# First mixer of a hybrid decoder: another order of the small products of the head pairs

## The chip, the cores and the metric

The kernel runs on one core of a Trainium2 chip. The metric is the device time of one execution in microseconds. Before the change it is 1539.14 us, the median of 3 runs (1536.59 to 1540.36).

## What is computed

The reference is one inference step of a two-layer trunk for two groups of requests that share the weights: one prompt of 512 positions and 8 sequences of 4 new positions each, 544 columns in all, 1024 channels. Every layer is a mixer and a feed-forward part, each with a layer norm behind it. The first mixer has two halves, a convolution module on 512 channels and a recurrence on the other 512, in 8 heads of 64:

```
p = x @ w_in                          # 1024 -> conv slice | recurrence slice
for each head and position t:         # the state s is 64 x 64
    sa = -s @ kk_t
    s  = s * decay_t + outer(sa, kk_t * a_t) + outer(v_t, k_t)
    y_t = s @ r_t
out = concat(ya, norm(y) * g) @ w_out
```

## The kernel before, in words

Channels lie on the 128 partitions, positions along the free axis. Weights stream in as f32, are split into a rounded high part and a rest (L262 on ScalarE, L170 on VectorE or GpSimd), and each projection is three products of split operands. All projections go through one helper, so their products have the line L192; L170 and L167 are helpers of VectorE and GpSimd (`tt`, `stt`), L164 one of ScalarE.

The recurrence of the 512 prompt positions is computed in 8 chunks of 64 positions. Two heads share the 128 partitions, one on partitions 0 to 63, the other on 64 to 127 (`HS[0]`, `HS[1]`): a head pair, of which there are four. Per pair there are these parts:

- `pair_in`: projections and element-wise work give `ar`, `kb` and `v`.
- `pair_front`, with `wkv_front` (L709) and `wkv_solve`. L725 multiplies `kb` and `ar` of each of 8 chunks and 2 heads: a contraction over the 64 partitions of one head, 128 rows and 128 columns of output. Four chunks fill one bank of PSUM, and VectorE multiplies the bank by a mask into `xa` and `xk`. SyncE's queue takes `xa` to DRAM (L730, `dx`), one transfer per half, and the solve reads it back in another layout (L770, `xb`). GpSimd inverts small triangles (`stmp`, `mm`), and the result goes through DRAM (L783, `dm`) into `mn` (L787). Meanwhile the front makes transposes and `R`.
- `pair_mid`, with `wkv_mid` (L791): products with `mn` (L801, the first that needs the solve), L809, L816, L823, L831, and last L840, which multiplies the inverse `n64` with `R`. In L840 the contraction and the output of a chunk both lie on the half `HS[c % 2]`. ScalarE copies the result into `R` (L842) and `wv` (L844). Then `wkv_tail` makes the chunks' transfer matrices (L859, L865).
- `pair_out`, with `wkv_scan` (L873): the states run through the chunks one after the other (L882), then L889 multiplies each chunk's state with `qt`, on partition half `H` for contraction and output, and a norm and a gate follow.

PSUM is allocated by kinds of bank: 3 "mm", 1 "wi", 1 "wf", 2 "wo", 1 "wb". Before the change the front uses "wf" alone, the middle and the tail use "wo", and L889 "wi". A bank is given out again when its last reader is through.

The parts are generators that `weave` (L172) takes turns with: for instance the front of pair 1 beside the middle of pair 0, the inputs of pair 2, a convolution projection and convolution taps on VectorE. Each generator has an offset of priority (front -6, middle and output -4, taps +8; lower goes first), and a scheduler fixes each engine's order before the program runs. An engine works through its order and waits where an operand or a bank is not there yet.

An f32 product is two instructions on TensorE, so every product counts twice in the profile.

Of the kernel before, what the change touches and what calls it, by code (L numbers as in the profile page):

```python
# [15 lines left out]
P = 128  # L16
# [76 lines left out]
HS = (slice(0, 64), slice(64, 128))  # L93
# [31 lines left out]
class Kernel:  # L125
# [583 lines left out]
    def wkv_front(self, d, dx):  # L709
        nc, gp = self.nc, self.gp  # L710
        ar, kb, v = d["ar"], d["kb"], d["v"]

        xa = d["xa"] = gp.tile([P, 2, 8, 64], F32, name="xa", tag="xa", bufs=XA)
        xk = d["xk"] = gp.tile([P, 2, 8, 2, 64], F32, name="xk", tag="xk", bufs=2)
        R = d["R"] = gp.tile([P, 2, 4, 2, 64], F32, name="R", tag="R", bufs=2)
        wv = d["wv"] = gp.tile([P, 2, 4, 2, 64], F32, name="wv", tag="wv", bufs=2)
        m3 = self.con0("ma").rearrange("p (a t) -> p a t", a=2).unsqueeze(1).broadcast_to([P, 4, 2, 64])
        idn = self.con("ident")
        flat = lambda t: t.rearrange("p a t -> p (a t)")
        for hd in range(2):  # L720
            for g in range(2):
                pa = self.bank([P, 4, 2, 64], "wf")
                for i in range(4):
                    c = 4 * g + i
                    nc.tensor.matmul(pa[:, i], lhsT=flat(kb[HS[hd], c // 2, c % 2]), rhs=ar[HS[hd], :, c], start=True,  # L725
                                     stop=True)
                for a, t in enumerate((xa[:, hd, 4 * g:4 * g + 4], xk[:, hd, 4 * g:4 * g + 4, 0])):
                    self.tt(t, pa[:, :, a], m3[:, :, a], ALU.mult)
            for c2 in range(2):
                nc.sync.dma_start(out=dx[HS[c2], hd * 4:hd * 4 + 4, :],  # L730
                                  in_=xa[HS[c2], hd].rearrange("p (cp c2) t -> p cp c2 t", c2=2)[:, :, c2])
            yield

        pt = self.bank([P, 4, 2, 64], "wf")
        for j in range(1, 4):
            nc.tensor.transpose(flat(pt[:, j]), v[:, 128 * j - 64:128 * j + 64], idn)
        nc.tensor.matmul(flat(pt[HS[1], 0]), lhsT=v[:, 0:64], rhs=idn, start=True, stop=True)
        nc.tensor.transpose(flat(pt[HS[0], 0]), v[:, 448:512], idn)
        for c2 in range(2):
            nc.scalar.copy(wv[HS[1 - c2], c2], pt[HS[1 - c2]])  # L740
        yield
        pb = self.bank([P, 2, 4, 64], "wf")
        for c, c2, cp, j, hd, S, O in self.blocks():
            nc.tensor.matmul(pb[S, hd, cp], lhsT=xa[O, hd, c], rhs=wv[O, c2, j, hd], start=True, stop=True)
        nc.scalar.copy(R[:, :, :, 1], pb)
        yield
        pt = self.bank([P, 4, 2, 64], "wf")
        for cp in range(4):
            nc.tensor.transpose(flat(pt[:, cp]), flat(ar[:, 0, 2 * cp:2 * cp + 2]), idn)
        nc.scalar.copy(R[:, :, :, 0], pt.rearrange("p cp hd c -> p hd cp c"))  # L750
        for g in range(2):
            pt = self.bank([P, 4, 2, 64], "wf")
            for i in range(4):
                c = 4 * g + i
                nc.tensor.transpose(flat(pt[:, i]), flat(kb[:, c // 2, c % 2]), idn)
            nc.scalar.copy(xk[:, :, 4 * g:4 * g + 4, 1], pt.rearrange("p c hd t -> p hd c t"))
        yield
# [33 lines left out]
    def wkv_mid(self, d):  # L791

        nc, gp = self.nc, self.gp
        mn = self.mn.rearrange("p (hd cp) a t -> p hd cp a t", hd=2)
        xa, R, wv = d["xa"], d["R"], d["wv"]
        S0, S1 = [slice(h, h + 32) for h in (0, 64)], [slice(h, h + 32) for h in (32, 96)]
        new = lambda nm, w, tag, bufs: gp.tile([P, 2, 4, w], F32, name=nm, tag=tag, bufs=bufs)
        all_ = list(self.blocks())
        pz = self.bank([P, 2, 4, 64], "wo")
        for c, c2, cp, j, hd, S, O in all_:  # L800
            nc.tensor.matmul(pz[S, hd, cp], lhsT=xa[S, hd, c], rhs=mn[S, hd, cp, 0], start=True, stop=True)  # L801
        z = new("z", 64, "s2k", S2)
        f = lambda t: t.rearrange("p hd cp t -> p (hd cp) t")
        self.tt(f(z), f(pz), self.con0("off16").unsqueeze(1).broadcast_to([P, 8, 64]), ALU.mult)
        yield

        pi = self.bank([P, 2, 4, 32], "wo")
        for c, c2, cp, j, hd, S, O in all_:
            nc.tensor.matmul(pi[S0[c2], hd, cp], lhsT=mn[S0[c2], hd, cp, 1, 0:32], rhs=z[S0[c2], hd, cp, 0:32],  # L809
                             start=True, stop=True)  # L810
        ni = new("ni", 32, "ni", 1)
        for q in S0:
            self.tt(ni[q], pi[q], mn[q, :, :, 0, 0:32], ALU.add)
        pn = self.bank([P, 2, 4, 64], "wo")
        for c, c2, cp, j, hd, S, O in all_:
            nc.tensor.matmul(pn[S, hd, cp], lhsT=z[S, hd, cp], rhs=mn[S, hd, cp, 1], start=True, stop=True)  # L816
        n64 = new("n64", 64, "n64", 1)
        self.tt(n64, pn, mn[:, :, :, 1], ALU.add)
        yield

        px = self.bank([P, 2, 4, 32], "wo")
        for c, c2, cp, j, hd, S, O in all_:
            nc.tensor.matmul(px[S1[c2], hd, cp], lhsT=xa[S0[c2], hd, c, 32:64], rhs=ni[S0[c2], hd, cp], start=True,  # L823
                             stop=True)
        x = new("x", 32, "nx", 1)
        for q in S1:
            nc.scalar.copy(x[q], px[q])
        yield
        po = self.bank([P, 2, 4, 32], "wo")
        for c, c2, cp, j, hd, S, O in all_:  # L830
            nc.tensor.matmul(po[S0[c2], hd, cp], lhsT=x[S1[c2], hd, cp], rhs=n64[S1[c2], hd, cp, 32:64], start=True,  # L831
                             stop=True)
        for q in S0:
            nc.scalar.copy(n64[q, :, :, 32:64], po[q])
        yield
        for h in range(2):
            pw = self.bank([P, 4, 2, 64], "wo")
            for c, c2, cp, j, hd, S, O in all_:
                if hd == h:
                    nc.tensor.matmul(pw[S, j].rearrange("p a t -> p (a t)"), lhsT=n64[S, h, cp],  # L840
                                     rhs=R[S, h, cp].rearrange("p a t -> p (a t)"), start=True, stop=True)
            nc.scalar.copy(R[:, h, :, 0], pw[:, :, 0])  # L842
            for c2 in range(2):
                nc.scalar.copy(wv[HS[c2], c2, :, h], pw[HS[c2], :, 1])  # L844
        yield
# [27 lines left out]
    def wkv_scan(self, p, d):  # L873
        nc, gp = self.nc, self.gp
        qt, gt, xp, pend = d["qt"], d["gt"], d["xp"], d["pend"]
        st = gp.tile([P, 9, 64], F32, name="st", tag="st", bufs=1)
        pss = self.bank([P, 8, 64], "wb")
        nc.gpsimd.tensor_copy(st[:, 1], xp[:, 0, 0])
        for c in range(1, 8):
            c2, cp = c % 2, c // 2  # L880
            for H in HS:
                nc.tensor.matmul(pss[H, c], lhsT=gt[H, c2, cp], rhs=st[H, c], start=True, stop=True)  # L882
            self.stt(st[:, c + 1], pss[:, c], pend[:, c:c + 1], xp[:, c2, cp], ALU.mult, ALU.add)
            yield
        nc.scalar.dma_start(out=self.O["wkv_p"][p], in_=st[:, 8])
        py = self.bank([P, 8, 64], "wi")
        for c in range(1, 8):
            for H in HS:
                nc.tensor.matmul(py[H, c], lhsT=st[H, c], rhs=qt[H, c % 2, c // 2], start=True, stop=True)  # L889
        y = d["y"][:, 64:NP]  # L890
        self.tt(y, py[:, 1:8].rearrange("p c t -> p (c t)"), y, ALU.add)
        yield
# [977 lines left out]
```

## Time and profile before

| | |
|---|---|
| median of 3 runs | 1539.14 us |
| the profiled execution | 1547.23 us, its span 1545.5 us |
| TensorE busy | 1449.8 us, 94% of the span |
| VectorE, ScalarE, GpSimd busy | 66%, 40%, 23% |
| mean granted TensorE clock | 0.951 of full speed |
| first mixer with its small products | roughly 40 to 370 us of the span |

The profile is of one execution. PE is TensorE, DVE VectorE, ACT ScalarE, POOL GpSimd, SP SyncE, which here only issues DMAs. An engine's share is an average over stages with different limits, so the views by stage are read for the stretch in which the change lies. Durations of neighbouring products on TensorE overlap, as they are pipelined; the distance of their starts is what a product takes of the engine's time.

### The profile page before, as it was taken

The page shows a single profiled execution, that of the slowest core. Times are in us where ns is not written, and L with a number is a line of the kernel's source. Part 1 is how long each engine was busy: PE and PEld are TensorE (multiplying, and loading weights), DVE is VectorE, ACT ScalarE, POOL GpSimd, SP SyncE. Part 2 cuts the span into 40 slices and gives each one's busy share as a digit, 9 for nine tenths or more (in the row PEclk, how much of TensorE's full clock was granted, in tenths as well). Part 3 has the DMA queues.
Part 4 walks back from the last instruction along what each step waited for, and adds up shares of the span by engine and source line. Part 5 has one row for each costly group of instructions (what it writes and reads, how often), then busy time and mean ns, then how long its engine had stood idle before and what let it go on. Part 6 is the DMA issues. An engine that isn't in the chain of part 4 may idle for free.

```text
span 1545.5 us, 31297 instructions
## 1 busy us (share of the span) xinstructions
PE 1449.8 (94%) x12064; PEld 1378.1 (89%) x12064; DVE 1016.7 (66%) x2513; ACT 617.1 (40%) x1407; POOL 353.5 (23%) x492
## 2 busy tenths in 40 slices
PE   7999999789799999999999789899999999999996
PEld 6987887577789999999999778799899999999996
DVE  6698786776979955558994856554675555554335
ACT  5444252251364444442233526443454444442222
POOL 1252542621540100003551611103420000000102
PEclk9999999799899999999999789899999999999997
DMA  5222123111313232225563278632222222233321
GB/s 189 74 63 70 39 53 101 22 38 57 101 44 117 87 123 89 90 86 165 175 184 111 98 209 218 176 101 97 74 63 95 89 87 87 89 91 86 84 68 58
DMA packets 128341, 152.43 MB, mean 99 GB/s; under 512 B 46513, under 2 KB 71857, under 8 KB 127937
## 3 DMA queue, kind: packets, MB, share of 16 engines
q1 hardware_dynamic: 105232, 120.11, 26.5%
q10 hardware_dynamic: 20800, 22.46, 4.7%
q0 software_dynamic: 2160, 7.87, 1.6%
q8 instruction: 95, 1.56, 0.4%
q14 instruction: 54, 0.43, 0.1%
HBM read 128.17 MB, written 22.22 MB: 97 GB/s over the span
## 4 chain that ended last, share of the span: by engine, by line
PE 71%; DVE 10%; DMA 6%; POOL 5%; issue 4%; ACT 3%; SPq 1%; ACTq 0%; POOLq 0%; DVEq 0%
PE ps_mm L192 61%; PE ps_wk L192 3%; POOL mm L170 2%; DVE xres L170 2%; POOL stmp L170 2%; DVE xres L167 1%; DVE wlo L170 1%; DMA tm<-dk 1%; PE ps_wf L725 1%; DMA ye<-dy 1%; DVE ln_t L167 1%; DMA xin<-in_xT 1%; POOL s5a L170 1%; PE ps_wk L1089 1%; ACT xres L164 1%
## 5 line engine op out<-in xcount | busy, mean ns | idle before, releaser
L192 PE MATMUL ps_mm<-xh,whi 128*128 128x256 f32 (+1 forms) x2016 | 492.2, 298 | 22.5 <-ACT whi L262 6.8
L192 PE MATMUL ps_mm<-xl,whi 128*128 128x256 f32 (+1 forms) x2016 | 493.5, 296 | 4.7 <-DVE xl L167 3.6
L192 PE MATMUL ps_mm<-xh,wlo 128*128 128x256 f32 (+1 forms) x2016 | 490.5, 295 | 0.0
L262 ACT CAST whi<-wraw 128x512 fp32r<-128x512 f32 x380 | 230.8, 611 | 517.9 <-PE ps_mm L192 445.6
L170 DVE TENSOR_TENSOR wlo<-wraw,whi 128x512 fp32r<-128x512 f32 x350 | 256.6, 735 | 271.3 <-ACT whi L262 266.2
L192 PEld LDWEIGHTS ps_mm<-xh,whi 128*128 128x128 f32 x2016 | 353.6, 195 | 30.3 <-ACT whi L262 7.1
L192 PEld LDWEIGHTS ps_mm<-xl,whi 128*128 128x128 f32 x2016 | 357.0, 195 | 13.6 <-issue 5.9
L192 PEld LDWEIGHTS ps_mm<-xh,wlo 128*128 128x128 f32 x2016 | 354.9, 194 | 4.6 <-issue 3.9
L192 PE MATMUL ps_mm<-fh,whi 128*128 128x256 f32 (+1 forms) x704 | 154.2, 290 | 0.0
L192 PE MATMUL ps_mm<-fl,whi 128*128 128x256 f32 (+1 forms) x704 | 153.2, 289 | 0.0
L192 PE MATMUL ps_mm<-fh,wlo 128*128 128x256 f32 (+1 forms) x704 | 153.0, 288 | 0.0
L192 PEld LDWEIGHTS ps_mm<-fh,whi 128*128 128x128 f32 x704 | 115.4, 188 | 1.8 <-issue 1.6
L192 PEld LDWEIGHTS ps_mm<-fh,wlo 128*128 128x128 f32 x704 | 115.7, 188 | 0.1
L192 PEld LDWEIGHTS ps_mm<-fl,whi 128*128 128x128 f32 x704 | 115.7, 188 | 0.0
L167 DVE SCALAR_TENSOR_TENSOR c<-ps_mm,cols,c 128x254 f32<-128x254 f32 (+3 forms) x264 | 98.3, 394 | 0.3
L167 DVE SCALAR_TENSOR_TENSOR cacc<-uext,cols,cacc 128x512 f32<-128x512 f32 x120 | 94.8, 790 | 2.5 <-ACT cacc L164 1.6
L170 POOL TENSOR_TENSOR ln_s<-xres 128x256 f32<-128x256 f32 (+1 forms) x8 | 10.8, 1368 | 312.6 <-DVE xres L170 312.6
L170 DVE TENSOR_TENSOR c<-ps_mm,c 128x256 f32<-128x256 f32 (+1 forms) x88 | 35.4, 436 | 59.2 <-PE ps_mm L192 54.8
L170 POOL TENSOR_TENSOR wlo<-wraw,whi 128x512 fp32r<-128x512 f32 x30 | 41.4, 1388 | 81.1 <-ACT whi L262 78.4
L192 PE MATMUL ps_mm<-yh,whi 128*128 128x256 f32 (+1 forms) x240 | 58.6, 299 | 0.3 <-ACT sg L164 0.3
L192 PE MATMUL ps_mm<-yl,whi 128*128 128x256 f32 (+1 forms) x240 | 57.4, 294 | 0.0
L192 PE MATMUL ps_mm<-yh,wlo 128*128 128x256 f32 (+1 forms) x240 | 57.4, 293 | 0.0
(374 smaller groups left out, 2085.6 us busy)
## 6 DMA issues: line engine op xcount, KB each, us to landing
wraw<-in_w_up SPq DMA_DIRECT2D x176, 256.0 KB
wraw<-in_w_down SPq DMA_DIRECT2D x80, 256.0 KB
wraw<-in_w_in_ab SPq DMA_DIRECT2D x44, 256.0 KB
wraw<-in_w_out_c SPq DMA_DIRECT2D x21, 256.0 KB
wraw<-in_w_out_ab SPq DMA_DIRECT2D x16, 256.0 KB
df<-s5a ACTq DMA_DIRECT2D x8, 512.0 KB
gx<-dg POOLq DMA_DIRECT2D x8, 512.0 KB, 4.9
tm<-dk SPq DMA_DIRECT2D x64, 64.0 KB
```

The costliest lines, as they stand in the source:

```text
L164: return self.nc.scalar.activation(out, in_, f, **k)
L167: return self.nc.vector.scalar_tensor_tensor(out, a, s, b, op0, op1)
L170: return (eng or self.nc.vector).tensor_tensor(out, a, b, op=op)
L192: ins = self.nc.tensor.matmul(*a, **k)
L262: self.nc.scalar.copy(hi, src)
L725: nc.tensor.matmul(pa[:, i], lhsT=flat(kb[HS[hd], c // 2, c % 2]), rhs=ar[HS[hd], :, c], start=True, stop=True)
L1089: gate = nc.tensor.matmul(pq[:, 4 * i + j:4 * i + j + 1], lhsT=t[:, b - P:b], rhs=self.con("ones")[:, 0:1], start=t is ts[0], stop=t is ts ...
```

## The change

Three places get another order. In `wkv_front` the two heads take turns, chunk by chunk, each with a bank of its own ("wf" and "wo"), so a round is eight products instead of four and there are two rounds per pair instead of four; both heads' transfers of `xa` to `dx` are issued in the second round. In `wkv_mid` the products of both heads are issued chunk by chunk into two "wo" banks, and the copies follow after all of them. In `wkv_scan` the chunks go in twos: two on one partition half, then the same two on the other.

```diff
-        for hd in range(2):
-            for g in range(2):
-                pa = self.bank([P, 4, 2, 64], "wf")
-                for i in range(4):
-                    c = 4 * g + i
+        for g in range(2):
+
+            pas = [self.bank([P, 4, 2, 64], t) for t in ("wf", "wo")]
+            for i in range(4):
+                c = 4 * g + i
+                for hd, pa in enumerate(pas):
                     nc.tensor.matmul(pa[:, i], lhsT=flat(kb[HS[hd], c // 2, c % 2]), rhs=ar[HS[hd], :, c], start=True,
                                      stop=True)
+            for hd, pa in enumerate(pas):
                 for a, t in enumerate((xa[:, hd, 4 * g:4 * g + 4], xk[:, hd, 4 * g:4 * g + 4, 0])):
                     self.tt(t, pa[:, :, a], m3[:, :, a], ALU.mult)
-            for c2 in range(2):
-                nc.sync.dma_start(out=dx[HS[c2], hd * 4:hd * 4 + 4, :],
-                                  in_=xa[HS[c2], hd].rearrange("p (cp c2) t -> p cp c2 t", c2=2)[:, :, c2])
+                if g:
+                    for c2 in range(2):
+                        nc.sync.dma_start(out=dx[HS[c2], hd * 4:hd * 4 + 4, :],
+                                          in_=xa[HS[c2], hd].rearrange("p (cp c2) t -> p cp c2 t", c2=2)[:, :, c2])
             yield
...
-        for h in range(2):
-            pw = self.bank([P, 4, 2, 64], "wo")
-            for c, c2, cp, j, hd, S, O in all_:
-                if hd == h:
-                    nc.tensor.matmul(pw[S, j].rearrange("p a t -> p (a t)"), lhsT=n64[S, h, cp],
-                                     rhs=R[S, h, cp].rearrange("p a t -> p (a t)"), start=True, stop=True)
+        pws = [self.bank([P, 4, 2, 64], "wo") for _ in range(2)]
+        for c, c2, cp, j, hd, S, O in all_:
+            nc.tensor.matmul(pws[hd][S, j].rearrange("p a t -> p (a t)"), lhsT=n64[S, hd, cp],
+                             rhs=R[S, hd, cp].rearrange("p a t -> p (a t)"), start=True, stop=True)
+        for h, pw in enumerate(pws):
             nc.scalar.copy(R[:, h, :, 0], pw[:, :, 0])
...
-        for c in range(1, 8):
+        for cs in ((1, 2), (3, 4), (5, 6), (7,)):
             for H in HS:
-                nc.tensor.matmul(py[H, c], lhsT=st[H, c], rhs=qt[H, c % 2, c // 2], start=True, stop=True)
+                for c in cs:
+                    nc.tensor.matmul(py[H, c], lhsT=st[H, c], rhs=qt[H, c % 2, c // 2], start=True, stop=True)
```

## Rows read from the trace of the kernel before

**Rows 1.** The page: busy time of each engine; TensorE in 40 slices, in tenths

```profile
PE 1449.8 (94%) x12064; PEld 1378.1 (89%) x12064; DVE 1016.7 (66%) x2513; ACT 617.1 (40%) x1407; POOL 353.5 (23%) x492
...
PE   7999999789799999999999789899999999999996
```

**Rows 2.** The chain of waits, 60 to 370 us: shares of that stretch

```profile
by line: PE ps_mm L192 28.9%; POOL mm L170 8.0%; POOL stmp L170 7.5%; issue 4.8%; PE ps_wf L725 4.5%; SPq L787 2.9%; PE ps_wo L840 2.5%; DMA dm<-mm 2.2%; DMA dx<-xa 1.8%; DMA mn<-dm 1.8%; PE ps_wo L801 1.8%; ACT L164 1.7%; PE ps_wb L882 1.6
```

**Rows 3.** Table by stage: length, busy us of each engine (instructions), granted clock, DMA

```profile
180.00:210.00 30.00, 30.00 (x356) 25.04 (x354) 26.77 (x50) 13.52 (x30) 8.37 (x13) 0.92 0.16 46
...
270.00:300.00 30.00, 21.33 (x234) 14.21 (x234) 25.81 (x55) 6.44 (x14) 21.09 (x39) 0.73 0.13 25
```

**Rows 4.** Waits of TensorE, 60 to 345 us: total, times, longest

```profile
PE ps_wo L801 <- DMA mn<-dm: 12.7, 5, 3.5
```

**Rows 5.** Groups of TensorE by shape: count, busy us, mean ns, idle before

```profile
L725 PE MATMUL ps_wf<-ar,kb 64*128 64x128 f32 x128 | 19.5, 288 | 0.0
...
L840 PE MATMUL ps_wo<-R,n 64*64 64x128 f32 x128 | 10.3, 302 | 0.0
...
L889 PE MATMUL ps_wi<-qt,st 64*64 64x64 f32 x112 | 6.0, 225 | 0.0
```

**Rows 6.** Timeline of TensorE, two front rounds: start, length, line, count

```profile
65.83 0.93 PE L725 MATMUL ps_wf<-ar,kb 64*128 64x128 f32 x6
...
70.22 0.30 PE L192 MATMUL ps_mm<-xl,whi 128*128 128x288 f32 x1
70.35 0.29 PE L192 MATMUL ps_mm<-xh,wlo 128*128 128x288 f32 x1
70.57 1.16 PE L725 MATMUL ps_wf<-ar,kb 64*128 64x128 f32 x8
71.66 0.40 PE L192 MATMUL ps_mm<-xh,whi 128*128 128x288 f32 x1
71.90 0.30 PE L192 MATMUL ps_mm<-xl,whi 128*128 128x288 f32 x1
```

**Rows 7.** Timeline of TensorE: whole groups of L840, L816 and L889

```profile
202.63 1.96 PE L840 MATMUL ps_wo<-R,n 64*64 64x128 f32 x30
...
251.70 1.20 PE L816 MATMUL ps_wo<-mn,z 64*64 64x64 f32 x32
...
272.20 1.03 PE L889 MATMUL ps_wi<-qt,st 64*64 64x64 f32 x28
```

**Rows 8.** Timeline of TensorE: last two front rounds of pair 0 and pair 3

```profile
76.22 1.16 PE L725 MATMUL ps_wf<-ar,kb 64*128 64x128 f32 x8
...
83.42 1.16 PE L725 MATMUL ps_wf<-ar,kb 64*128 64x128 f32 x8
...
264.71 1.16 PE L725 MATMUL ps_wf<-ar,kb 64*128 64x128 f32 x8
...
268.75 1.16 PE L725 MATMUL ps_wf<-ar,kb 64*128 64x128 f32 x8
```

**Rows 9.** Timelines of VectorE and SyncE: last xa multiply and its transfers, pair 0

```profile
85.29 0.42 DVE L170 TENSOR_TENSOR xa<-ps_wf,cons 128x256 f32<-128x256 f32 x1
...
85.73 1.25 SPq L730 DMA_DIRECT2D dx<-xa  x2
```

**Rows 10.** Timeline of ScalarE: copies behind L840, first and second head

```profile
203.75 0.37 ACT L842 COPY R<-ps_wo 128x256 f32<-128x256 f32 x1 [0.89 <-PE ps_wo L840]
...
204.79 0.37 ACT L842 COPY R<-ps_wo 128x256 f32<-128x256 f32 x1
```

**Rows 11.** Timelines of TensorE and VectorE: a front round between two middle groups

```profile
193.59 0.46 PE L823 MATMUL ps_wo<-ni,xa 32*32 32x32 f32 x16
...
195.51 1.16 PE L725 MATMUL ps_wf<-ar,kb 64*128 64x128 f32 x8
...
197.48 0.71 PE L831 MATMUL ps_wo<-n,x 32*32 32x32 f32 x32
...
197.79 0.41 DVE L170 TENSOR_TENSOR xk<-ps_wf,cons 128x256 f32<-128x256 f32 x1
```

## The prediction

> **What bounds the kernel now.** I read the page first. TensorE is busy for 94% of the span, VectorE for 66%; in the slices the 9s of TensorE break between slice 7 and slice 10, roughly 270 to 425 us [rows 1]. The products that the change touches all lie in the first mixer, so next comes the chain of waits of that stretch, 60 to 370 us. The plain projections (L192) hold the largest share; L725, the first of the three edited products, holds 4.5% of 310 us, some 14 us; the rest of the chain is the triangular solve on GpSimd (stmp and mm) with the transfers around it [rows 2]. The table by stage shows the two regimes: TensorE busy 30.00 of 30 us at 180 to 210, but 21.33 of 30 at a granted clock of 0.73 at 270 to 300 [rows 3]. The list of waits names the one stall of weight inside: the first product of the middle part (L801) waits 12.7 us in 5 waits, at most 3.5 each, for the solve's result to land [rows 4]. So up to about 270 us a nanosecond saved on TensorE counts, unless the solve of the head pair comes no earlier; then it returns as waiting at L801.
>
> **The change, part by part.** The listing by shape gives the size: 128 instructions for L725, 128 for L840, 112 for L889 (an f32 product is two of them, so 64, 64 and 56 products) [rows 5].
>
> *Front products (L725).* Now a round is four products, 8 instructions, all on one half of the array's rows, into one bank. Such a round lasts 1.16 us, one of 6 instructions 0.93, so one more costs (1.16 - 0.93) / 2 = 0.115 us. What it takes out of the stream of projections is more: from the projection before it (70.35) to the second one behind it (71.90) is 1.55 us, where two steps of 0.13 would do, so 1.29 us; 8 x 0.115 = 0.92 of it is the products and 0.37 the going in and out [rows 6]. There are 16 rounds, 20.6 us. Afterwards there are 8 rounds of 16 instructions, whose neighbours use opposite halves of the rows and different banks. The trace shows no two products that differ in rows alone, so I bound it. From below in gain: nothing overlaps, a round costs 1.29 + 0.92 = 2.21 us, and 8 save 20.6 - 17.7 = 2.9. From above: it goes as the nearest row does, L840 today, whose neighbours differ in rows and in columns: 30 instructions in 1.96 us, (1.96 - 0.27) / 29 = 0.058 each [rows 7]; then 16 take 0.27 + 15 x 0.058 = 1.14 us, what 8 take now, and 8 rounds save 8 x 1.29 = 10.3. I take 10.3, as L840 is the same width of 128 on the same half of the rows; only its weights are half as wide.
>
> But the second bank is of kind "wo", which the middle part of the pair before also uses. Where none is free, the second head's products come after the first's and the round costs 2.21. Pair 0 has no middle part beside it; of the six rounds of pairs 1 to 3 I take two so, 2 x 0.92 = +1.8 us (bounds 0 and 5.5). VectorE's 32 multiplies of this part stay as many.
>
> *The transfers of head 0* move from the second round to the last, so four of them, not two, stand in SyncE's queue behind the last multiply, ahead of the reloads of the solve and of weight loads: two take 1.25 us, so +1.25, and the last xa multiply comes third instead of first, 2 x 0.42 = +0.84. Against it, two rounds go: the last one lay 7.2 us behind the one before in pair 0 (76.22 to 83.42) and 4.0 in pair 3 (264.71 to 268.75) [rows 8, 9]. The solve's input is thus ready about 2 to 5 us earlier per pair, and TensorE about 2 us earlier: I leave the wait at L801 as it is, 0. That stall is what is late next: the bounds are -6 (about half of the 12.7 goes) and +5 (4 x 1.25, if the rounds win nothing).
>
> *Middle products (L840).* Today opposite halves alternate in one bank; afterwards two products of the same half follow each other, then two of the other, in two banks. The trace has this order, with half the width, in L816: 32 instructions in 1.20 us, (1.20 - 0.22) / 31 = 0.0316 each, against (1.03 - 0.22) / 27 = 0.0300 for L889, which alternates at the same width [rows 7]. So 0.0016 more, twice that at full width: 128 x 0.0032 = +0.4 us. The bounds: no overlap left at all, 128 x (0.115 - 0.058) = +7.3; below, a break inside a group saved per pair, 4 x 0.37 = -1.5. The Trainium skill, page "TensorEngine Tiling (Array Packing)", section "Gotcha 1: PSUM Pressure", says that different row tiles cannot use one bank at the same time. By that rule today's L840, in one bank, would run one by one and a bank each would win 7.3 us; the 0.058 us a step of L840 stands against it, so the sum holds no such gain and the rule's result is a rival with a small chance.
>
> ScalarE's copies out of the first bank (L842, L844; about 1 us from 203.75 to the second set at 204.79) now begin after nearly all 32 instructions instead of 16, 16 x 0.058 = 0.9 us later [rows 10]; who waits is the tail (L859), with projections before it: 0, bounds 0 and 4 x 0.9 = 3.7.
>
> *Output products (L889).* The same step from turns to twos, one bank: 112 x 0.0016 = +0.2; if the overlap went, 112 x 0.029 = +3.2 (half of L840's 0.057).
>
> The sum: -10.3 + 1.8 + 0.4 + 0.2 = -7.9 us. It is made against the profiled execution, 1547.23 us (span 1545.5), which stands 8.1 above the median; a term of this size changes by nothing that matters between them, so 1539.14 - 7.9 = 1531.2 us.
>
> **The rivals.** *Row halves alone do not overlap*, or a "wo" bank is so seldom free that the order is not what the code says. Then -2.9 + 0.6 = -2.3: 1536.8. For it: no row shows such a pair. Against: the pairs of L840 and L889.
>
> *The wait for the solve goes too.* The input is earlier by more than TensorE is, and half of the 12.7 us goes: -7.9 - 6 = -13.9: 1525.2. For it: the distance of the rounds. Against: the solve on GpSimd stands between other work.
>
> *Slower: the front holds a bank of the middle.* The place is "wo", two banks. A round of the front holds its bank until VectorE has read it: 195.51 to 198.20 now, 2.7 us, and 3.5 with two more multiplies ahead; with one bank left, each product group of the middle waits for the evacuation of the last, and TensorE, which works in order, stands. At 2.5 us in each of six rounds that is +15: 1539.1 - 7.9 + 15 = 1546.2. It decides from 7.9 / 6 = 1.3 us a round. Against it: between two groups of the middle lie 3.4 us of other work (194.05 to 197.48) [rows 11], in which the bank comes free.
>
> *The twos lose their overlap.* Both upper bounds come true, 7.3 + 3.2 = 10.5 in place of 0.6: -10.3 + 1.8 + 10.5 = +2.0: 1541.1. Against: the 0.0316 of L816 in that order. The Trainium skill, page "TensorE: Matmul & The Clock Gate", section "Part 3: Packing small matmuls", says that a weight load overlaps a running product only if its row group differs, which speaks against the twos; by that rule this rival would be the likeliest, and L816 does not bear it out.
>
> *A bank each wins in the middle products*, because sharing one holds them apart today: -7.3 in place of +0.4, so -10.3 + 1.8 - 7.3 + 0.2 = -15.6: 1523.5. Against: the step of 0.058 in one bank, half of the 0.115 of products that don't overlap. This is the rule of the page on array packing named above.
>
> **How the numbers follow.** Forecast 0.55; row halves alone do not overlap 0.18; the wait goes too 0.11; the middle's bank held 0.10; the twos 0.04; a bank each wins 0.02. A measurement of this kernel tells about 0.3%, 4.6 us, from no change: below 1534.5 is faster, above 1543.8 slower. The forecast's own bounds put about 0.47 of its 0.55 below 1534.5; with 0.11, 0.02 and 0.03 of the first rival's, 0.63 faster. Slower is most of the held bank's case: 0.09. The rest, 0.28, is the same. The range 1523 to 1541 holds the forecast, the first rival and most of the second; it leaves out the held bank's case, half of the twos' and the edge of the gains.
>
> **What would show it.** Right: L725 in groups of up to 16 in about 1.2 us; two rounds per pair; L840 as 32 in about 2 us, L889 as 28 in about 1.1; the waits at L801 near 12; the first mixer ends about 8 us earlier. Wrong: 16 of L725 in about 2.1 us (row halves); a new wait of TensorE at L809, L816, L823, L831 or L840 for an xa or xk multiply (the bank); L840 or L889 at twice the time (the twos); L801 waiting longer than now, with dx issued later (the transfers).

## The result, and the profile after

The changed kernel takes 1553.45 us (median, 1550.56 to 1556.67) against 1539.75 us for the kernel before (1536.59 to 1544.0), measured side by side: a ratio of 1.0084, 95% interval 1.0059 to 1.0109. It is slower by some 13 us, where 8 us less had been forecast, and it lies outside the range. The profiled execution of before stood some 8 us above its median and that of after (1550.56 us) 3 below, so the two traces differ by 3.3 us only; they are compared stretch by stretch, not end to end.

The page of the changed kernel, busy time and TensorE in 40 slices, answers to [rows 1]:

```profile
PE 1439.2 (93%) x12064; PEld 1372.8 (89%) x12064; DVE 1012.0 (65%) x2513; ACT 616.6 (40%) x1407; POOL 343.5 (22%) x492
...
PE   7989897789879999999999789899899999999996
```

TensorE is busy for 10.6 us less (1439.2 against 1449.8) and the kernel is longer all the same: the engine is idle instead. Between 77 and 271 us three of the slices of TensorE lose one or two tenths. Where the loss is made can be told by counting the projections (L192) through: the 1400th starts at 419.0 us, where it started at 409.0, so some 10 us are lost in the first mixer. The table by stage, with the two stretches of [rows 3] and one between (length, busy us of each engine, granted clock, share of the DMA engines, GB/s):

```profile
180.00:210.00 30.00, 30.00 (x352) 26.59 (x351) 29.59 (x57) 12.71 (x29) 10.20 (x15) 1.00 0.25 71
240.00:270.00 30.00, 19.95 (x186) 16.31 (x184) 28.26 (x66) 4.02 (x7) 4.40 (x6) 0.66 0.30 88
270.00:300.00 30.00, 20.00 (x306) 15.04 (x304) 15.64 (x34) 8.71 (x22) 18.46 (x41) 0.83 0.11 20
```

and the row of 240 to 270 us in the kernel before:

```profile
240.00:270.00 30.00, 28.31 (x353) 24.29 (x354) 20.66 (x49) 7.32 (x17) 6.01 (x8) 0.89 0.39 112
```

At 240 to 300 us TensorE is busy for 39.95 of 60 us at a granted clock of 0.66 and 0.83; in the same stretch of before it is busy for 49.64 (28.31 and 21.33). So a third of the time is idle, and the clock falls towards its lower level (1.2 GHz) behind the pauses.

The list of waits of TensorE, 60 to 345 us, answers to [rows 4]:

```profile
PE ps_wf L758 <- ACT xk L759: 7.6, 1, 7.6
PE ps_wf L726 <- POOL kb L170: 7.1, 2, 5.4
PE ps_wo L804 <- DMA mn<-dm: 6.2, 3, 3.1
PE ps_wf L726 <- DVE xk L170: 3.7, 1, 3.7
```

The wait for the solve (L801, now L804) is halved, 6.2 us where 12.7 stood, but the front's products now wait for their operand `kb` from GpSimd and for their bank, and a transpose of the front (L758) waits 7.6 us for ScalarE. One thing is missing in this list, and it is the main one: no wait of L812, the first product behind L804, is in it. It shows only in the timeline. TensorE, pair 0's middle and pair 1's front:

```profile
104.14 0.44 PE L804 MATMUL ps_wo<-mn,xa 64*64 64x64 f32 x4
106.03 1.14 PE L804 MATMUL ps_wo<-mn,xa 64*64 64x64 f32 x28
...
124.49 0.37 PE L726 MATMUL ps_wf<-ar,kb 64*128 64x128 f32 x1 [1.66 <-POOL kb L170]
124.50 0.37 PE L726 MATMUL ps_wo<-ar,kb 64*128 64x128 f32 x1
124.70 0.27 PE L726 MATMUL ps_wf<-ar,kb 64*128 64x128 f32 x1
124.71 0.27 PE L726 MATMUL ps_wo<-ar,kb 64*128 64x128 f32 x1
124.91 0.71 PE L812 MATMUL ps_wo<-z,mn 32*32 32x32 f32 x32
```

and two of VectorE's rows, the one that makes the operand of L812 and the first that reads the front's "wo" bank:

```profile
107.28 0.69 DVE L170 TENSOR_TENSOR z<-ps_wo,cons 128x512 f32<-128x512 f32 x1
...
128.96 0.41 DVE L170 TENSOR_TENSOR xa<-ps_wo,cons 128x256 f32<-128x256 f32 x1
```

In the kernel before, the same place of pair 0, TensorE and then VectorE:

```profile
123.78 1.14 PE L801 MATMUL ps_wo<-mn,xa 64*64 64x64 f32 x28
...
131.69 0.31 PE L809 MATMUL ps_wo<-z,mn 32*32 32x32 f32 x6
...
125.33 0.68 DVE L170 TENSOR_TENSOR z<-ps_wo,cons 128x512 f32<-128x512 f32 x1
```

`z` is there at 107.97, yet L812 starts at 124.91, 17 us later (5.7 before), right behind the first two products of the front, which waited for `kb`. My reading, which the experiments below test: the front, whose priority is better (-6 against -4), asks for a "wo" bank first, and L812 gets a place behind it in TensorE's fixed order. What L812 lacked was not a free bank: it runs at 124.91, while VectorE reads the front's "wo" bank only at 128.96, so it used the other one. It is the place in the order that holds it. In between TensorE goes on with projections (111 instructions of L192, counted in the trace between the last L804 and the first L812; before it was 36), so nobody "waits" in the profile: the middle is simply late. Pairs 1 and 2 show the same with 114 and 38 (31 and 23 before): there too L812 starts 17 us behind `z`, at 190.64 and 253.49, right behind the first two products of the front. From the start of the first L804 to the start of the last product of L841 (L840 before), the middles of pairs 0, 1 and 2 last 43.7, 45.3 and 44.2 us; before 32.2, 27.1 and 25.6. Pair 3, which has no front beside it, is shorter than before: 20.1 against 24.2.

The three edited groups, by shape, answer to [rows 5]:

```profile
L726 PE MATMUL ps_wf<-ar,kb 64*128 64x128 f32 x64 | 11.9, 328 | 10.8 <-POOL kb L170 7.1 <-DVE xk L170 3.7
L726 PE MATMUL ps_wo<-ar,kb 64*128 64x128 f32 x64 | 11.7, 327 | 0.0
L841 PE MATMUL ps_wo<-R,n 64*64 64x128 f32 x128 | 8.2, 274 | 0.0
L892 PE MATMUL ps_wi<-qt,st 64*64 64x64 f32 x112 | 6.8, 233 | 0.7 <-ACT xres L164 0.7
```

and the timeline of whole groups of L841 and L892 answers to [rows 7]:

```profile
146.04 2.01 PE L841 MATMUL ps_wo<-R,n 64*64 64x128 f32 x32
...
227.34 1.08 PE L892 MATMUL ps_wi<-qt,st 64*64 64x64 f32 x28 [0.72 <-ACT xres L164]
```

These are as forecast: L841 steps by (2.01 - 0.27) / 31 = 0.056 us (0.058 before), L892 by (1.08 - 0.22) / 27 = 0.032 (0.030 before).

How the loss reaches the end: pair 2's middle is through at 278.2 instead of 266.2, so its transfer matrices and the scan behind them come later, in a stretch in which the projections have been used up. The first projection behind that stretch, in the changed kernel and then in the kernel before:

```profile
335.90 0.39 PE L192 MATMUL ps_mm<-xh,whi 128*128 128x256 f32 x1 [1.41 <-ACT xh L262]
```

```profile
321.18 0.58 PE L192 MATMUL ps_mm<-xh,whi 128*128 128x256 f32 x1 [2.20 <-ACT xh L262]
```

The last one ahead of it starts at 242.6 us in the changed kernel and at 258.5 before, so TensorE is without projections for 93.3 us instead of 62.7.

### The profile page after: what moved, and what is told of

Same layout as the page of the kernel before. It is cut to its first block, busy times and chain, and to the rows that moved or that the text cites. A ratio compares the mean times of both kernels' runs of the same rounds, so it can differ in the third digit from the quotient of the medians.

```text
span 1548.7 us, 31302 instructions
## 1 busy us (share of the span) xinstructions
PE 1439.2 (93%) x12064; PEld 1372.8 (89%) x12064; DVE 1012.0 (65%) x2513; ACT 616.6 (40%) x1407; POOL 343.5 (22%) x492
## 4 chain that ended last, share of the span: by engine, by line
PE 65%; DVE 10%; DMA 3%; ACT 3%; issue 2%; POOL 1%; SPq 0%; ACTq 0%; DVEq 0%; POOLq 0%
PE ps_mm L192 58%; PE ps_wk L192 3%; DVE xres L170 2%; DVE xres L167 1%; DMA tm<-dk 1%; ACT xres L164 1%; DVE cacc L167 1%; DVE ln_t L167 1%; DMA dy<-yg 1%; PE ps_wk L1092 1%; DVE wlo L170 1%; DMA ye<-dy 1%; DMA wraw<-in_w_in_c 0%; DVE s5b L170 0%; ACT xh L164 0%
## 5 line engine op out<-in xcount | busy, mean ns | idle before, releaser
L192 PE MATMUL ps_mm<-xh,whi 128*128 128x256 f32 (+1 forms) x2016 | 492.6, 299 | 26.1 <-ACT whi L262 6.5
L192 PE MATMUL ps_mm<-xl,whi 128*128 128x256 f32 (+1 forms) x2016 | 492.9, 296 | 4.7 <-DVE xl L167 3.4
L192 PE MATMUL ps_mm<-xh,wlo 128*128 128x256 f32 (+1 forms) x2016 | 490.6, 295 | 0.0
L192 PEld LDWEIGHTS ps_mm<-xh,whi 128*128 128x128 f32 x2016 | 353.7, 195 | 37.0 <-issue 8.8
L192 PEld LDWEIGHTS ps_mm<-xl,whi 128*128 128x128 f32 x2016 | 357.7, 195 | 10.4 <-DVE xl L167 4.3
L192 PEld LDWEIGHTS ps_mm<-xh,wlo 128*128 128x128 f32 x2016 | 355.4, 194 | 2.2 <-issue 1.7
L192 PE MATMUL ps_mm<-fh,whi 128*128 128x256 f32 (+1 forms) x704 | 154.4, 290 | 0.0
L192 PE MATMUL ps_mm<-fl,whi 128*128 128x256 f32 (+1 forms) x704 | 153.5, 289 | 0.0
L192 PE MATMUL ps_mm<-fh,wlo 128*128 128x256 f32 (+1 forms) x704 | 153.3, 289 | 0.0
L192 PEld LDWEIGHTS ps_mm<-fh,whi 128*128 128x128 f32 x704 | 115.6, 188 | 1.8 <-issue 1.6
L192 PEld LDWEIGHTS ps_mm<-fh,wlo 128*128 128x128 f32 x704 | 115.9, 189 | 0.1
L192 PEld LDWEIGHTS ps_mm<-fl,whi 128*128 128x128 f32 x704 | 115.9, 188 | 0.0
L192 PE MATMUL ps_mm<-yh,whi 128*128 128x256 f32 (+1 forms) x240 | 58.0, 296 | 0.3 <-ACT sg L164 0.3
L192 PE MATMUL ps_mm<-yh,wlo 128*128 128x256 f32 (+1 forms) x240 | 57.2, 292 | 0.0
L192 PE MATMUL ps_mm<-yl,whi 128*128 128x256 f32 (+1 forms) x240 | 56.9, 292 | 0.0
```

What stands on the lines that cost most here:

```text
L192: ins = self.nc.tensor.matmul(*a, **k)
```

## The experiments

The theory was that the order in which "wo" is asked for costs the time: the front asks first and holds the bank until GpSimd has made `kb`, and the middle of the pair before stands behind it. The rivals were the two other parts of the change, the front's two rounds themselves (operands and transfers wanted in one go), a stop of ScalarE's queue seen in the trace, and mere luck of the schedule. "Middles" below is the sum over pairs 0 to 2 of the length defined above, read from each timeline; "covered" is TensorE's busy time in 240 to 300 us, from the table by stage.

| kernel | time, us | ratio to before, 95% | middles, us | covered, us |
|---|---|---|---|---|
| before | 1539.75 | | 84.9 | 49.64 |
| changed | 1553.45 | 1.0084 [1.0059, 1.0109] | 133.2 | 39.95 |
| e1 front part only | 1552.5 | 1.0079 [1.0049, 1.0108] | 131.9 | 40.95 |
| e2 the other two parts only | 1543.23 | 1.0014 [0.9993, 1.0035] | 82.6 | 52.20 |
| e3 front, head 1 in "wb" | 1543.82 | 1.0015 [0.9993, 1.0036] | 76.4 | 50.49 |
| e4 changed, state load on SP | 1559.26 | 1.0101 [1.0065, 1.0136] | 133.7 | 37.59 |
| e5 front, three turns later | 1535.97 | 0.9960 [0.9933, 0.9987] | 79.2 | 49.48 |
| e6 as e3, heads not in turns | 1545.92 | 1.0033 [1.0005, 1.0061] | 72.0 | 46.67 |
| e7 as e3, sums on VectorE | 1538.99 | 0.9985 [0.9955, 1.0015] | 80.4 | 48.75 |
| e8 before, sums on VectorE | 1559.39 | 1.0119 [1.0066, 1.0171] | 79.2 | 49.62 |
| e9 before, three turns later | 1546.43 | 1.0032 [1.0006, 1.0059] | 87.4 | 52.77 |
| e10 changed, three turns later | 1543.16 | 1.0005 [0.9988, 1.0021] | 76.6 | 52.00 |
| e11 four rounds, head 1 in "wo" | 1548.97 | 1.0037 [1.0006, 1.0068] | 113.1 | 43.07 |
| e12 front, two turns later | 1540.82 | 0.9979 [0.9959, 0.9999] | 92.5 | 51.28 |
| e13 e5 and turns in L841 | 1534.26 | 0.9932 [0.9908, 0.9957] | 76.7 | 53.08 |
| e14 e5 and twos | 1536.23 | 0.9961 [0.9932, 0.9990] | 86.4 | 52.36 |
| e15 as e5, heads not in turns | 1540.14 | 0.9978 [0.9956, 1.0001] | 84.7 | 45.46 |
| e16 e5 again | 1534.61 | 0.9954 [0.9927, 0.9982] | 81.7 | 49.58 |

The kernel before ran beside each set at medians of 1539.75 to 1543.07 us; the ratio is to those, so kernels of different sets (changed; e1 to e4; e5 to e8; e9 to e12; e13 to e16) are compared by their ratios.

### Which part: e1 and e2

The first takes the front's hunk of the diff alone, the second the hunks of L840 and L889 alone.

> Only the front's part of the change: two rounds, head 0 in 'wf', head 1 in 'wo'; L840 and L889 as in the kernel before. Bank-order theory: everything that was lost is here, 1548 to 1558 us, and the projections between the last of L801 and the first of L809 in pairs 0 to 2 stretch as in the changed kernel. Theory that the shared rounds of L840 and the twos cost it: within 4 us of the kernel before (1536 to 1543).

> Only the other two parts: L840's two banks filled in turns, L889's chunks in twos; the front as before. Bank-order theory: 1537 to 1543 us (0 to +3). Theory that these two parts cost it: 1548 us or more.

The front alone is the whole loss (1.0079 against 1.0084), with 111, 106 and 66 instructions of L192 between L804 and L812. The other two parts alone make no measurable difference.

### Is it the bank: e3 and e11

```diff
-            pas = [self.bank([P, 4, 2, 64], t) for t in ("wf", "wo")]
+            pas = [self.bank([P, 4, 2, 64], t) for t in ("wf", "wb")]
```

> The front's two rounds, but head 1 in the single 'wb' bank (that of the broadcast rows) in place of 'wo'; rest as before. Bank-order theory: the middle's requests for 'wo' no longer stand behind the front, the middle of pairs 0 to 2 lasts 22 to 32 us again and the time is 1528 to 1541 us. Theory that the two-round front itself (its operands wanted in one go, its transfers in one go) costs the time, whatever the bank: 1548 us or more.

The middles are short again (27.8, 26.6 and 22.0 us) and the loss is gone: the two-round front does not cost the time, its place in "wo" does. But nothing is gained on the kernel before either, and the time is 3 us over the range expected. The waits of TensorE in this run, 60 to 345 us, show what came in its place:

```profile
PE ps_wf L758 <- ACT xk L759: 5.4, 2, 4.7
PE ps_wo L834 <- ACT x L830: 3.5, 1, 3.5
PE ps_wo L804 <- DMA mn<-dm: 3.2, 1, 3.2
```

The 4.7 us lie at 213 to 218 us. ScalarE's timeline at that place:

```profile
217.38 0.23 ACT L164 ACTIVATE pexs<-xres 128x32 f32<-128x32 f32 x1 [5.07 <-POOL xres L170]
217.40 0.35 ACTq L977 DMA_DIRECT2D s<-in_wkv  x1
217.52 0.21 ACT L164 ACTIVATE rps<-xres 128x32 f32<-128x32 f32 x1
217.64 0.56 ACT L759 COPY xk<-ps_wf 128x512 f32<-128x512 f32 x1
```

The copy L759, which frees the front's bank, stands behind an activation that waits for three small additions on GpSimd, and GpSimd is in the middle of the solve of pair 2, which came 10 us earlier than before (its first row at 206.42 us, 216.02 before). The part that is earlier meets the part that isn't.

The mirror of e3 keeps four rounds and every order of before and moves only head 1's rounds to "wo":

```diff
-                pa = self.bank([P, 4, 2, 64], "wf")
+                pa = self.bank([P, 4, 2, 64], ("wf", "wo")[hd])
```

> The kernel before, four rounds a pair and all orders as before, but head 1's two rounds in 'wo'. Bank-order theory: here L809 and L816 stand ahead of the front, but L823 (the product after them) stands behind it, so the middle of pairs 0 to 2 lasts 35 to 45 us and the time is 1547 to 1557 us. Theory that the loss comes from the two rounds or the turns of the heads: 1538 to 1545 us.

Here L809 and L816 run early and L823, the next to ask, is the one that stands behind the front: 94, 82 and 54 instructions of L192 between L816 and L823 (14, 7 and 10 before). Its median is 7 us over the kernel before and inside what was expected, though its runs spread over 1534 to 1554 and its trace is of the slowest. The stall moves to whichever product asks behind the front, with no change of the rounds' code.

### Is it the order of the requests: e5, e12, e9, e16

The front keeps "wo" but begins three turns of `weave` later (for pairs 1 to 3), so that it asks behind the middle:

```diff
-        weave((hi, pair_mid(0)), (md, pair_front(1)), ...
+        weave((hi, pair_mid(0)), (md, after(3, pair_front(1))), ...
```

> Front part of the change, head 1 in 'wo' as changed, but the fronts of pairs 1 to 3 begin three turns later, so that their request for 'wo' stands behind the middle's L809 and L816. Bank-order theory (the order of the requests, not the bank as such, is what costs): the middle of pairs 0 to 2 lasts 22 to 35 us again, and the time is 1536 to 1548 us. If sharing 'wo' costs whatever the order, or the last pair's later front shows at the end: 1549 us or more.

> As the run with the front three turns later, but two turns: L834 now stands behind the front in pairs 0 and 1 (64 and some 40 projections between L826 and L834). Bank-order theory: between the two, the middle of pairs 0 and 1 at 30 to 42 us and 1539 to 1550 us. If only the first requests (L812, L819) matter: 1533 to 1539 us.

TensorE's timeline of e5 in the same place as above, and VectorE's row for `z`:

```profile
105.25 1.14 PE L804 MATMUL ps_wo<-mn,xa 64*64 64x64 f32 x28
110.67 0.24 PE L812 MATMUL ps_wo<-z,mn 32*32 32x32 f32 x2
...
111.86 0.69 PE L812 MATMUL ps_wo<-z,mn 32*32 32x32 f32 x30
112.49 1.14 PE L819 MATMUL ps_wo<-mn,z 64*64 64x64 f32 x28
...
115.52 0.71 PE L826 MATMUL ps_wo<-ni,xa 32*32 32x32 f32 x32
119.11 0.71 PE L834 MATMUL ps_wo<-n,x 32*32 32x32 f32 x32
124.40 0.37 PE L726 MATMUL ps_wf<-ar,kb 64*128 64x128 f32 x1
```

```profile
106.43 0.69 DVE L170 TENSOR_TENSOR z<-ps_wo,cons 128x512 f32<-128x512 f32 x1
```

The front's products start at 124.40, as in the changed kernel (124.49, where they waited for `kb`), so the front loses nothing in pair 1. But in the meantime four groups of the middle have run. With three turns the kernel is at 0.996 of before, and again 0.995 in e16; with two turns, where L834 still stands behind the front (64 and 37 instructions of L192 between L826 and L834 in pairs 0 and 1), at 0.998. Three settings of one number give 1552.5, 1540.8 and 1536.0 us with middles of 131.9, 92.5 and 79.2.

> Control: the kernel before with the fronts of pairs 1 to 3 three turns later, nothing else. Theory that the gain over the kernel before in the run with the later front is that of the two-round front: 1538 to 1546 us, no gain. Theory that the later start alone brings it: 1533 to 1538 us.

> The front part with the later start once more, as the base for the three others on this chip: 1533 to 1539 us.

The same later start without the two-round front makes the kernel before slower (1.0032), so it is no gain of its own. Between e9 and e5, which differ by the front part alone, stand 10.5 us; the ratio of the two ratios, 0.9960 / 1.0032 = 0.9928, says 11. That is what the front part (a second bank, two rounds and the turns together) is worth where it asks behind the middle.

### What it is not: e4, e7, e8

In the changed kernel ScalarE's queue stood for 9.69 us at 276 to 286 us, the one place where its copies were plainly blocked. Its timeline there:

```profile
276.05 0.41 ACT L517 COPY yb<-ps_wi 128x288 f32<-128x288 f32 x1
285.76 0.34 ACTq L977 DMA_DIRECT2D s<-in_wkv  x1
286.14 0.59 ACT L759 COPY xk<-ps_wf 128x512 f32<-128x512 f32 x1 [9.69 <-POOL yb L170]
```

A load of the sampled state waits for a buffer that GpSimd frees late, and the copies stand behind it. The edit moves that load to SP's queue:

```diff
-            nc.scalar.dma_start(out=s0[p], in_=self.I["wkv"][:, p])
+            nc.sync.dma_start(out=s0[p], in_=self.I["wkv"][:, p])
```

> The changed kernel with the sampled state's load (L977) issued by SP in place of ScalarE, so that ScalarE's queue no longer stands for 9.7 us at 276 to 286 us behind GpSimd. ScalarE-queue theory: 6 to 12 us less than the changed kernel, 1541 to 1548 us. Bank-order theory alone (the third pair is late anyway, and the queue is only where it shows): within 3 us of the changed kernel.

L759 and the copies run at once and the tail of pair 2 is 7 us earlier (its first product, L861, at 281.5 instead of 288.1), yet the kernel isn't faster (1.0101 against 1.0084, with intervals that overlap; by the medians 6 us slower, more than either theory allowed); the stall has moved to the solve's transfers, by TensorE's waits in 60 to 345 us:

```profile
PE ps_wo L804 <- DMA mn<-dm: 16.6, 4, 12.5
```

So e4 alone doesn't settle it, as it put one stall in the place of another. What speaks against the theory of ScalarE's queue are two kernels without the loss: in e10 the copies stand behind the same load for 6.41 us, in e13, whose median is the lowest of all, for 4.59.

The next two move the three additions of e3's stall from GpSimd to VectorE, once with the front in its own bank and once in the kernel before:

```diff
-                self.tt(ss_[...], ss_[...], ss_[...], ALU.add, nc.gpsimd)
+                self.tt(ss_[...], ss_[...], ss_[...], ALU.add)
```

> As the own-bank run, with the three additions on 128x8 (the sampled columns' running sums) on VectorE in place of GpSimd, where in the own-bank run they stood behind the solve of pair 2 (ScalarE waited 5.1 us for them at 212 us and TensorE 4.7 us for ScalarE, half clock behind it). If the lead of the front is lost there: 4 to 9 us under the own-bank run, 1535 to 1540 us. If the lead goes anyway (the last pair's operands): within 3 us of it.

> Control: the kernel before with the same three additions on VectorE. No wait of TensorE for ScalarE's L756 stands at that place in its trace, so nothing is expected: 1537 to 1545 us, within 3 us of the kernel before, by either theory.

With its own bank the front gains about 5 us by it (1538.99 against 1543.82; the intervals overlap, so it is a hint and no proof). The control missed badly: the kernel before is 17 us slower by an edit of twelve tiny additions. Its middles are no longer and its covered time is that of before, so this is another loss: pair 3's front starts at 257.9 and ends at 277.2 us, where it ran from 255.0 to 269.6. Why this is so was not tried. It says that in this kernel a reshuffle of the fixed order alone can cost 1%, and that no single pair of runs here proves a cause; what carries the verdict is that e1, e3, e5, e11 and e12 move the stall to the product that the request's place names, and that the time without projections goes with it: 93.3 us in the changed kernel, 89.8 in e1 and 82.9 in e11, against 62.7 before, 70.2 in e3, 65.4 in e5, 68.2 in e12 and 68.4 in e10. The control e8 is between, at 78.4.

### What is left: e10, e13, e14, and e6, e15

> The whole change (front, turns in L841, twos in L892) with the fronts of pairs 1 to 3 three turns later. Bank-order theory: as the front part with the later start, 1533 to 1542 us; the loss of the change is gone. If the other two parts cost something beside it: 1545 us or more.

> Front part with the later start, and the middle's last products (L841) of both heads in turns into two 'wo' banks; L889's chunks singly. If this part takes the 7 us of the whole change (both banks are wanted at once, the copies of head 0 follow all 32 products): 1541 to 1546 us. If not: 1534 to 1539 us.

> Front part with the later start, and the chunks of the scan's products in twos; L840 as before. By the starts read so far twos cost 0.05 us per pair: 1534 to 1539 us. If they take the 7 us: 1541 to 1546 us.

The later start takes the loss out of the whole change too (1.0005), but the 6 us that the front alone gains are missing. Neither of the other parts takes them: with the turns in L841 alone the kernel has the lowest median of all (1534.26 us, 0.9932), with the twos alone it is as e5. From 120 to 228 us the projections (L192) of e10 and e13, counted through, run within 0.4 us of each other; they part in the stretch of pair 3's middle and the last scan, where the two fixed orders differ: the 1100th projection starts at 335.1 us in e10 and at 328.2 in e13. Both parts together give a worse order there; why the scheduler makes it stays open.

e6 and e15 put head 0's four products ahead of head 1's in each round:

```diff
-            for i in range(4):
-                c = 4 * g + i
-                for hd, pa in enumerate(pas):
+            for hd, pa in enumerate(pas):
+                for i in range(4):
+                    c = 4 * g + i
```

> As the own-bank run, but within a round the four products of head 0 come first and then the four of head 1, each in its own bank. If two heads in turns overlap and that is worth the 9 us that the front lost of its busy time, the rounds take 2.3 to 2.6 us in place of 1.2 to 1.4 and the time is 5 to 10 us over the own-bank run (1549 to 1554). If what the front saves on TensorE never reaches the end, because the last pair waits for its operands: 1540 to 1547 us, within 3 us of the own-bank run.

> Front part with the later start, but in each round head 0's four products stand before head 1's. If the overlap of the two row halves is worth what the distances of the starts say (0.06 against 0.11 to 0.13 us an instruction over 256 instructions, some 8 to 10 us in part beside other work): 1540 to 1547 us. If a second bank and two rounds are all that counts: 1534 to 1539 us.

Both miss their purpose: where both banks are free, the scheduler sets the heads in turns all the same. TensorE's timeline of e15:

```profile
124.43 0.37 PE L726 MATMUL ps_wf<-ar,kb 64*128 64x128 f32 x1
124.44 0.37 PE L726 MATMUL ps_wo<-ar,kb 64*128 64x128 f32 x1
```

The products of L726, overlaps counted once, keep TensorE busy for the same time in e15 and e16 (sum of the four stretches that hold the fronts, the table by stage with that line alone; e15 first, then e16):

```profile
sum 85.00, PE 15.89 PEld 13.02; mean PE 3.97 PEld 3.26
```

```profile
sum 80.00, PE 15.84 PEld 12.78; mean PE 3.96 PEld 3.19
```

So what the turns are worth was not measured by these two; e15's 5 us over e16 lie within the two intervals. On TensorE e12 shows it better, below.

## Why the prediction was wrong, point by point

**What bounds the kernel.** Right: TensorE up to some 250 us, the middle and the solve after that. A saving on TensorE is there, 10.6 us of busy time by the page (L726 accounts for 3.1 of it, below; the rest was not followed up), and it did not shorten the kernel.

**Front products, -10.3.** The mechanism was right and the size wrong. Row halves alone do overlap: in turns, the starts lie 0.01 and 0.10 us apart (above, 124.70 and 124.71), and 12 instructions run in 0.67 us from first start to last. But only somewhat over half of them go so. In three of the four pairs of the changed kernel the second round ran as eight of one bank and then eight of the other, as the banks come free one after the other. Overlaps counted once, L726 takes 16.44 us in the changed kernel and 15.84 in e5, where L725 took 19.54. In the changed kernel pair 1, nearly all in turns, takes 2.92 us, and pair 3 takes 6.57 at half the clock (0.50); every pair of the kernel before takes 4.88. The rows of pair 1, of pair 3 and the sum over the pairs:

```profile
120.00:140.00 20.00, 2.92 (x32) 2.35 (x32) 0.91 0.19 56
...
250.00:270.00 20.00, 6.57 (x32) 5.42 (x32) 0.50 0.29 82
sum 80.00, PE 16.44 PEld 13.57; mean PE 4.11 PEld 3.39
```

and the sum in e12, where seven of the eight rounds go in turns at least in part:

```profile
sum 80.00, PE 11.87 PEld 9.76; mean PE 2.97 PEld 2.44
```

So the term was worth 3.1 us of TensorE in the changed kernel, near its lower bound of 2.9, and 7.7 where the turns hold. That e5 stands 10 us under e9, as if the term had come true, is luck: it is due in part to something that the forecast had put down as "2 to 5 us earlier per pair" and priced at 0. With one bank each of the four rounds comes behind VectorE's reading of the one before; with two banks the front of pair 0 lasts 5.5 us (62.2 to 67.7) in the changed kernel instead of 19.7 (64.6 to 84.3), and the first L804 of pairs 0 to 2 comes 15.0, 9.5 and 6.6 us earlier. It is the second bank that does this: in e11, with four rounds, the first L801 comes as early, at 104.3, 165.9 and 227.4 us.

**The step that failed** is the one that begins "But the second bank is of kind "wo", which the middle part of the pair before also uses". It charged the front with +1.8 us (bounds 0 and 5.5) for its own lost overlap and the middle with nothing. The measured time is 13 us up where 8 down were forecast, some 21 us apart; between e1 and e5, which differ by the three turns alone, stand 16.5 us (1.0079 against 0.9960). What the runs showed in the step's place: the front's earlier request puts L812 behind the front's first products in TensorE's order, the middles of pairs 0 to 2 last 133.2 us in place of 84.9, and the projections run out 16 us earlier.

**The rival of the held bank** (chance 0.10, +15, 1546.2 us) named the place and the sign. Its mechanism was half right. It let the front hold the bank for the time of a round, until VectorE has read it, 2.7 to 3.5 us, and argued against itself with the 3.4 us of other work between two groups [rows 11]. In the trace of the changed kernel the middle is not held by a bank in use, but by its place behind products that wait for their operand: 17 us in pair 0, because the front's `kb` comes from GpSimd. That the place goes with the shared kind of bank and with who asks first is shown by e3, e5, e11 and e12; by what rule the scheduler makes it is not shown. And TensorE does not stand; it uses up the projections that were to cover the end of the mixer, so that the price is paid at 240 to 335 us, far from the cause. The sign that the prediction had set for this rival, a new wait of a middle product for an xa or xk multiply, is therefore not in the list of waits.

**The wait at L804** went from 12.7 to 6.2 us, the gain that the second rival had named, and was buried by the above. **The transfers of head 0** show no cost: the four of pair 0 leave SP from 66.35 us on, the last at 71.60, where the last two left from 85.73 on [rows 9].

**Middle products, copies and twos** (+0.4, 0, +0.2): as forecast, by the steps of 0.056 and 0.032 us and by e2, but for one new wait of the tail for the copies (L861 in pair 3, 2.4 us), inside the bound of 3.7. Two rules had been weighed there. The Trainium skill, page "TensorEngine Tiling (Array Packing)", section "Gotcha 1: PSUM Pressure", says that different row tiles can't use one bank at the same time. By it a rival of the prediction let a bank each win 7.3 us. The change gives a bank to each head, and both halves still write to it; L841 steps by 0.056 us where L840 stepped by 0.058 in one bank, and in that one bank the instructions of L840 started in pairs, 7 ns apart and 110 ns from pair to pair, where those of L725 follow one by one at 112 ns, so the trace does not bear the rule out. The Trainium skill, page "TensorE: Matmul & The Clock Gate", section "Part 3: Packing small matmuls", has a weight load overlap a running product only if the row group differs. L892 in twos steps by 0.032 us where it stepped by 0.030 alternating, so no loss of that kind shows in this order.

**The chances.** 0.09 on slower was too little, mainly because the middle's cover was judged by the time between two groups and not by who asks first for the bank.

## What to carry to other kernels

Where an order is fixed before the program runs, borrowing a bank can put the lender's next product behind the borrower's first ones, and there it waits for the borrower's operands even if a bank is free: before a second bank is borrowed, compare the time at which its operands exist with that at which the lender needs the bank, and ask behind the lender if it is sooner. Such a stall was in no list of waits here, since the engine went on with other work; measure the length of the part between its first and last product, and count what stands between two dependent groups. And try a neutral reshuffle as a control before 1% is put down to a cause: here one cost 17 us.

## What the runs showed that was not expected

- Products that differ in their row half alone, each in its own bank, overlap nearly whole: pairs start 0.01 us apart and follow every 0.10 to 0.11 us, so one instruction costs some 0.055 us instead of 0.11.
- A pause of a few us can be paid twice: behind the 4.7 us wait of e3 the stretch of 215 to 225 us has a granted clock of 0.66, and the L192 products there take 0.44 us instead of 0.30:

```profile
215.00:225.00 10.00, 6.74 (x53) 6.35 (x54) 3.60 (x8) 4.07 (x8) 8.13 (x27) 0.66 0.32 93
```

- The lowest median is that of the front part with the later start and the turns in L841 (e13), 1534.26 us, 0.9932 of before with an interval of 0.9908 to 0.9957: it beats both the kernel before and the change. From e5, e14 and e16 its interval doesn't part it.
